# Seven block products in place of eight for six more groups of a SwiGLU layer, in a two-layer trunk on one core

## The chip, the core and the metric

The kernel runs on one core of a Trainium2 chip. Its engines are TensorE (PE; its weight loads are listed apart as PEld), VectorE (DVE), ScalarE (ACT), GpSimd (POOL) and SyncE (SP), which issues most transfers. The metric is the time of one execution in device microseconds (us), lower is better.

## The reference, cut to what matters

Two layers; each is half a SwiGLU, a mixer, half a SwiGLU. The sequence has 256 rows (two tiles of 128), the model 1024 columns, the SwiGLU 2816 hidden columns.

```python
def _swiglu(h, w_gate, w_up, w_down):
    return (jax.nn.silu(h @ w_gate) * (h @ w_up)) @ w_down

for layer in range(DEPTH):
    x = x + 0.5 * _swiglu(_rmsnorm(x, ffn_norm[layer, 0]), ffn_w_gate[layer, 0],
                          ffn_w_up[layer, 0], ffn_w_down[layer, 0])
    h = _rmsnorm(x, mix_norm[layer])
    ...
    x = x + mixed.astype(x.dtype)
    x = x + 0.5 * _swiglu(_rmsnorm(x, ffn_norm[layer, 1]), ffn_w_gate[layer, 1],
                          ffn_w_up[layer, 1], ffn_w_down[layer, 1])
```

So there are four SwiGLUs, which the kernel numbers f = 0 to 3. The mixer behind f = 0 is an attention with rotary tables (cosines and sines of the positions) beside pooling groups.

## The kernel before, in words

**Precision.** Every product is made of three fp32r products: a matrix is split into a high part (ACT copies it to fp32r, `hi_of`) and a low part (DVE subtracts, `tt`), and high x high, high x low and low x high are added in PSUM. So each weight costs ACT one pass and DVE one pass before PE can use it. The splits are written to `wh` and `wl`, a ring of four units (RING); the transfers land in `raw`, four buffers. A unit is half of a group's gate and up columns (512 rows of the model by 256 + 256 columns) or a group's rows of `ffn_w_down`.

**Groups.** The hidden columns go in 11 groups of 256 (g = 0 to 10). For a group, `gate_up` makes for each tile t and each half kh of the model's columns 12 products of 128 x 512 (4 blocks by 3 terms) into one PSUM buffer `wk`; ACT takes the silu (`sg`), DVE multiplies (`pr`). `hid_T` transposes `pr` on PE into a PSUM buffer `sk` and splits it (`hh`, `hl`); `down` adds 12 products for each tile into the accumulators `acc`. `wk` and `sk` have two buffers each. The step of a group (`ffn_joint`) is: four times 12 products of gate and up; `down` of the group before for tile 0; `hid_T`; `down` of the group before for tile 1.

**Pairs.** `ffn_pairs` treats two neighbouring groups together: tiles, halves of the model's columns and the two groups make 2 x 2 blocks, and seven products of blocks (`pair_product`, j = 1, 6, 2, 7, 5, 4, 3 in that order) replace eight. Its rows are sums of blocks of the normalised rows, scaled by `rho` so that both tiles share a scale (`pair_rows`, eight or four passes of DVE), and are transposed by 16 PE transposes (`pair_turn`) into `sTh`, `sTl`. Its weights come raw into `sr` (four buffers, one pair's worth); `split_pair` makes sums and differences of them on DVE (into `sr` and `t2`) and splits the seven results, each in two parts. After each product DVE or ACT adds it into `u`; a gate's result is `pp`. Before, `PAIRS = {3: (2, 5, 8)}`: only f = 3 does this, for groups 2 and 3, 5 and 6, 8 and 9.

**Order.** A scheduler decides the order on each engine from the steps' order and priorities; each engine then runs its list strictly in that order. `opened` (a step behind group 3 of f = 0) loads the mixer's constants and makes the rotary tables, some 58 small DVE instructions (names `rt..`, `rang`, `posf`, `cs`).

Of the kernel before, what the change touches and what calls it, by code (L numbers as in the profile page):

```python
# [17 lines left out]
DM = 1024  # L18
# [21 lines left out]
    p510 m1 t00 p500 v00 t11 p411 p511 G1 p501 v10 G0 t13 v01 v11 V0 V1 o20 o21 o31 o30  # L40
"""

PAIRS = {3: (2, 5, 8)}


ORDER = """
# [66 lines left out]
def trunk_kernel(ctx: ExitStack, tc: tile.TileContext, I, out):  # L113
# [341 lines left out]
    def gate_up(f, g, t, kh, ks):  # L455

        w = held["f", f, g, kh]
        o = slice(t * 128, (t + 1) * 128)
        if (f, g, t) not in gups:
            gups[f, g, t] = wk((128, 2, 256))  # L460
        ps = gups[f, g, t]

        sides = [slice(0, 1), slice(1, 2)] if (f, g, t, kh) == (0, 0, 0, 0) else [slice(0, 2)]
        for sd in sides:
            for x, y in ((hTh, w[0]), (hTh, w[1]), (hTl, w[0])):
                for k in ks:
                    keep("gu", mm(ps[:, sd], x[:, 4 * kh + k, o], y[:, k, sd],
                                  kh == 0 and k == 0 and y is w[0] and x is hTh and sd.start == 0,
                                  kh == 1 and k == 3 and x is hTl))
                if x is hTh and y is w[0]:  # L470
                    pins["up"] = pins["gu"]
        if kh == 0 or ks[-1] != 3:
            return
        del gups[f, g, t]
        sg = tmp.tile([128, 256], F32, tag="t256", name="sg")
        pr = tmp.tile([128, 256], F32, tag="pr256", name="pr")
        with prio(CHAIN):
            ACT.activation(out=sg, in_=ps[:, 0], func=AF.Silu, scale=rstds[f, t])  # L478
            stt(pr, ps[:, 1], rstds[f, t], sg, ALU.mult, ALU.mult)
        prods[f, g, t] = pr  # L480
# [12 lines left out]
    def pair_rows(f):  # L493

        a11, a12, a21, a22 = (hn[t][:, c * 512:(c + 1) * 512] for t in range(2) for c in range(2))
        rho = pr_["rho"]
        if f == 0:
            gv = pr_["pool"].tile([128, DM], F32, name="pg")
            SP.dma_start(out=gv, in_=I["ffn_norm"][0, 0].partition_broadcast(128))
            for t in range(2):  # L500
                for c in range(2):
                    o = slice(c * 512, (c + 1) * 512)
                    tt(hn[t][:, o], xs[t][:, o], gv[:, o], ALU.mult)
        root = pr_["pool"].tile([128, 1], F32, name="root")
# [56 lines left out]
    def hid_T(f, g, *ts):  # L561
# [3 lines left out]
                         hidp.tile([128, 2, 256], F32R, tag="hl", name="hl"))  # L565
        o = slice(ts[0] * 128, (ts[-1] + 1) * 128)
        h, l = (x[:, :, o] for x in hid[f, g])
        ps = sk((128, 2, len(ts) * 128))
        with prio(CHAIN), behind("down" if g else "gu"):
            for n, t in enumerate(ts):  # L570
                pr = prods.pop((f, g, t))
# [16 lines left out]

    at = {}

    def even_open():
        at["pool"] = p = tc.alloc_tile_pool(name="even", bufs=1)
        for nm, c0, n in (("NA", C_NA, 128), ("NB", C_NB, 256),
                          ("corr", C_CR, 64), ("invf", C_IF, 8)):
            at[nm] = p.tile([128, n], F32, name=nm)
            SP.dma_start(out=at[nm], in_=cst[:, c0:c0 + n])
        at["pw"] = p.tile([128, 4, 128], F32, name="pw")
        SP.dma_start(out=at["pw"], in_=I["ev_pool_w"][0].rearrange("g c e -> c g e"))
        at["psc"] = p.tile([128, 4], F32, name="psc")
        SP.dma_start(out=at["psc"], in_=I["ev_pool_scale"][0].rearrange("(g e) -> e g", e=128))  # L600
        at["gqk"] = p.tile([128, 2, 64], F32, name="gqk")
        SP.dma_start(out=at["gqk"][:, 0], in_=I["ev_q_norm"][0].partition_broadcast(128))
        SP.dma_start(out=at["gqk"][:, 1], in_=I["ev_k_norm"][0].partition_broadcast(128))
        at["pos"] = p.tile([128, 2], I32, name="pos")
        SP.dma_start(out=at["pos"], in_=I["positions"][0].rearrange("(t p) -> p t", p=128))
        at["qk"] = [p.tile([128, 2, 8, 64], F32, name=f"qk{t}") for t in range(2)]
        at["v"] = [p.tile([128, 8, 65], F32, name=f"v{t}") for t in range(2)]
        for t in range(2):
# [11 lines left out]
            at[nm] = [p.tile([128, 8], F32, name=f"{nm}{t}") for t in range(2)]  # L620
        at["att"] = [p.tile([128, 8, 64], F32, name=f"att{t}") for t in range(2)]
        at["plT"] = [p.tile([128, 4, 128], F32, name=f"plT{t}") for t in range(2)]
        at["cs"] = p.tile([128, 2, 2, 2, 8], F32, name="cs")
        at["ra"] = p.tile([128, 8, 2, 8], F32, name="ra")
        for nm in ("s8", "r8"):
            at[nm] = [p.tile([128, 8], F32, name=f"{nm}{n}") for n in range(2)]
# [89 lines left out]
        tt(cos, z, u, ALU.mult)  # L716

    def rotary_tables():
        p = at["pool"]
        posf = p.tile([128, 2], F32, name="posf")  # L720
        ang = p.tile([128, 2, 8], F32, name="rang")
        DVE.tensor_copy(out=posf, in_=at["pos"])
# [696 lines left out]
    def ffn_joint(f, g0, g1):  # L1419

        for g in range(g0, g1):
            paced.add(len(steps))
            for kh in range(2):
                if f == 1 and g == NG - 1 and kh:
                    S(hold)
                for t in range(2):
                    GU(f, g, t, kh)
                    if g == 1 and kh == 0:
                        HID(f, 0, t)
                    if g == 1 and f in PAIRS:  # L1430
                        S(lambda n=2 * kh + t: pair_turn(n))
            if g < NG - 1:
                dn(f, g - 1, 0)
# [3 lines left out]
    def ffn_pairs(f, g0, g1):  # L1437

        g = g0
        while g < g1:  # L1440
# [70 lines left out]


    def first():
        row = hn[1][0:8, 0:128]
        with prio(3 * CHAIN):
            ACT.dma_start(out=ident, in_=cst[:, C_ID:C_ID + 128])
# [55 lines left out]
    S(lambda: table(AF.Silu, "hT"))  # L1572
    GU(0, 0, 0, 1)
    GU(0, 0, 1, 1)
    ffn_joint(0, 1, 4)

    def opened():
        with behind("load"):
            load_g("m0", I["mix_norm"][0])
            even_open()  # L1580
        rotary_tables()
    S(opened)
    ffn_joint(0, 4, NG)
    tail(0, N(0, "m0"), HT(0))
    S(lambda: norm(1, "m0"))

# [37 lines left out]
    PO(1, 1, (1,))  # L1624
    C(x_update, 1, None, (1,))
    C(table, AF.Silu)
    S(lambda: at["pool"].release())
    S(s5_open)
    head(1, "f1")
    S(lambda: gens.append(s5_build()))  # L1630
# [144 lines left out]
```

## Time and profile before

| | |
|---|---|
| median of 3 runs | 937.63 us (936.35 to 939.73) |
| the profiled execution | 937.66 us |
| its span, first to last instruction | 935.9 us |
| PE busy | 914.7 us, 98% of the span |
| PEld busy | 755.9 us, 81% |
| DVE busy | 711.3 us, 76% |
| ACT busy | 464.9 us, 50% |
| mean granted TensorE clock | 0.998 of full speed |

Busy time of PE is a sum over pipelined matmuls whose ends are modelled: a matmul's duration overlaps its successor's. How fast PE runs is read from the starts of successive rows. In the rows, an idle time in brackets is what the engine waited before the row, and for whom.

### The profile page before, as it was taken

How to read it: one execution, taken by the hardware profiler on the slowest of the kernel's cores; microseconds unless marked ns; L12 is line 12 of the kernel's file. 1: busy time of each engine (PE TensorE's matmuls, PEld its weight loads, DVE VectorE, ACT ScalarE, POOL GpSimd, SP SyncE). 2: the span in 40 equal slices, each digit the busy share in tenths (PEclk: the TensorE clock that was granted, in tenths of full speed). 3: DMA queues.
4: the chain of work that ended last, by engine and by line, in shares of the span. 5: the costliest groups of instructions: out<-in, count | busy, mean ns of one | idle time of the engine just before them, and what ended most of it. 6: DMA issues, size and time to landing. Idle time of an engine off the chain costs nothing.

```text
span 935.9 us, 13253 instructions
## 1 busy us (share of the span) xinstructions
PE 914.7 (98%) x4981; PEld 755.9 (81%) x4981; DVE 711.3 (76%) x1141; ACT 464.9 (50%) x643; POOL 64.9 (7%) x114
## 2 busy tenths in 40 slices
PE   7999999999999999999999999999879999999998
PEld 5888888889988888888888888888658788887876
DVE  5756654578967659999896557999496689999992
ACT  6544444455536444434454444444345465656561
POOL 0000000013020000000132001600200000000000
PEclk9999999999999999999999999999999999999999
DMA  7867656654476877556788655865956941939141
GB/s 249 276 193 219 192 183 200 193 166 142 134 193 202 197 228 209 174 154 209 235 240 295 191 180 165 250 206 183 301 217 194 333 148 47 335 101 320 53 134 46
DMA packets 149055, 184.59 MB, mean 197 GB/s; under 512 B 23160, under 2 KB 131648, under 8 KB 148224
## 3 DMA queue, kind: packets, MB, share of 16 engines
q1 hardware_dynamic: 145184, 174.70, 60.0%
q0 software_dynamic: 3504, 8.92, 3.8%
q8 instruction: 39, 0.64, 0.3%
q10 hardware_dynamic: 304, 0.14, 0.1%
q14 instruction: 24, 0.20, 0.1%
HBM read 173.24 MB, written 9.44 MB: 195 GB/s over the span
## 4 chain that ended last, share of the span: by engine, by line
PE 76%; DVE 9%; DMA 7%; ACT 3%; issue 3%; POOL 1%; SPq 0%; ACTq 0%; DVEq 0%; POOLq 0%
PE wk L103 46%; PE acc L103 25%; PE sk L103 5%; DMA raw<-in_ffn_w_up_dram 3%; DVE wl L141 3%; DMA raw<-in_s_w_glu_dram 2%; ACT wh L184 1%; DMA V<-x 1%; DVE X L141 1%; DVE b_t L141 1%; POOL r L742 1%; DMA raw<-in_ffn_w_gate_dram 1%; ACT acc L383 0%; ACT h L1211 0%; DVE b_q L141 0%
## 5 line engine op out<-in xcount | busy, mean ns | idle before, releaser
L141 DVE TENSOR_TENSOR wl<-raw,wh 128x1024 fp32r<-128x1024 f32 (+1 forms) x281 | 335.1, 1217 | 119.6 <-ACT wh L184 118.7
L184 ACT ACTIVATE wh<-raw 128x1024 fp32r<-128x1024 f32 (+1 forms) x281 | 285.6, 1051 | 216.0 <-PE wk L103 94.5
L103 PE MATMUL wk<-wh,hTh 128*128 128x512 f32 (+1 forms) x776 | 203.1, 380 | 3.0 <-DVE pr L150 1.5
L103 PE MATMUL wk<-wl,hTh 128*128 128x512 f32 (+1 forms) x776 | 200.2, 377 | 0.0
L103 PE MATMUL wk<-wh,hTl 128*128 128x512 f32 (+1 forms) x776 | 199.4, 376 | 0.0
L103 PEld LDWEIGHTS wk<-wh,hTh 128*128 128x128 f32 x776 | 139.6, 189 | 30.2 <-ACT hTh L184 2.5
L103 PEld LDWEIGHTS wk<-wl,hTh 128*128 128x128 f32 x776 | 140.8, 189 | 26.5 <-DVE wl L141 0.2
L103 PEld LDWEIGHTS wk<-wh,hTl 128*128 128x128 f32 x776 | 140.8, 189 | 26.4
L103 PE MATMUL acc<-wh,hh 128*128 128x512 f32 x352 | 141.4, 402 | 1.4 <-ACT hh L184 1.4
L103 PE MATMUL acc<-wl,hh 128*128 128x512 f32 x352 | 137.2, 390 | 0.0
L103 PE MATMUL acc<-wh,hl 128*128 128x512 f32 x352 | 137.0, 392 | 0.0
L478 ACT ACTIVATE sg<-wk,rstd 128x256 f32<-128x256 f32 x76 | 35.8, 472 | 95.1 <-PE wk L103 90.5
L103 PEld LDWEIGHTS acc<-wh,hh 128*128 128x128 f32 x352 | 66.2, 188 | 14.8 <-ACT hh L184 2.7
L103 PEld LDWEIGHTS acc<-wh,hl 128*128 128x128 f32 x352 | 66.1, 188 | 14.8 <-DVE hl L141 0.7
L103 PEld LDWEIGHTS acc<-wl,hh 128*128 128x128 f32 x352 | 66.3, 188 | 12.4
L150 DVE SCALAR_TENSOR_TENSOR pr<-wk,rstd,sg 128x256 f32<-128x256 f32 x76 | 36.4, 480 | 35.9 <-ACT sg L478 35.9
L141 DVE TENSOR_TENSOR wl<-sr,wh 128x1024 fp32r<-128x1024 f32 x36 | 42.8, 1219 | 2.6 <-ACT wh L184 2.6
L184 ACT ACTIVATE hh<-sk 128x512 fp32r<-128x512 f32 (+1 forms) x52 | 27.4, 527 | 29.6 <-PE sk L103 29.6
L184 ACT ACTIVATE wh<-sr 128x1024 fp32r<-128x1024 f32 x36 | 36.2, 1052 | 11.5 <-PE acc L103 5.2
L141 DVE TENSOR_TENSOR hl<-sk,hh 128x512 fp32r<-128x512 f32 (+1 forms) x52 | 31.3, 604 | 4.3 <-ACT hh L184 4.3
L383 ACT ACTIVATE acc<-x 128x512 f32<-128x512 f32 x24 | 14.3, 597 | 22.6 <-DVE x L150 18.3
L103 PE MATMUL sk<-ident,pr 128*128 128x128 f32 x152 | 24.4, 273 | 0.3 <-DVE pr L150 0.3
(322 smaller groups left out, 819.7 us busy)
## 6 DMA issues: line engine op xcount, KB each, us to landing
raw<-in_ffn_w_down_dram SPq DMA_DIRECT2D x88, 512.0 KB
raw<-in_ffn_w_up_dram SPq DMA_DIRECT2D x76, 512.0 KB
raw<-in_ffn_w_gate_dram SPq DMA_DIRECT2D x75, 512.0 KB
raw<-in_ev_w_in_dram SPq DMA_DIRECT2D x16, 512.0 KB
raw<-in_s_w_glu_dram SPq DMA_DIRECT2D x16, 512.0 KB
sr<-in_ffn_w_gate_dram SPq DMA_DIRECT2D x12, 512.0 KB
sr<-in_ffn_w_up_dram SPq DMA_DIRECT2D x12, 512.0 KB
raw<-in_ev_w_out_dram SPq DMA_DIRECT2D x8, 512.0 KB
```

The lines of the kernel that those rows point to most:

```text
L103: i = f(*a, **k)
L141: return DVE.tensor_tensor(out=o, in0=a, in1=b, op=op)
L150: return DVE.scalar_tensor_tensor(out=o, in0=a, scalar=s, in1=b, op0=op0, op1=op1)
L184: return ACT.activation(out=o, in_=i, func=AF.Copy)
L383: keep("square", ACT.activation(out=into or acc_of(t)[c], in_=xs[t][:, s], func=AF.Square, scale=1.0 / 32.0, accum_out=sums[t][:, c:c + 1]))
L478: ACT.activation(out=sg, in_=ps[:, 0], func=AF.Silu, scale=rstds[f, t])
L742: POOL.tensor_tensor(out=r8, in0=s8, in1=mhalf.to_broadcast([128, 8]), op=ALU.pow)
```

## The change

`PAIRS` gets an entry for f = 0: groups 3 and 4, 6 and 7, 9 and 10 are paired; groups 0, 1, 2, 5 and 8 stay single. `pair_rows(0)` is a step behind group 0, so its instructions lie in groups 0 and 1; the four `pair_turn` of f = 0 lie in group 2. For f = 0 the rows aren't in `hn` as rows, so `pair_rows` loads the norm's gain to all partitions (`gv`, 512 KB, now in the buffer `gvec`) and multiplies again. Group 1's gate and up go to `sk` buffers instead of `wk`, and group 0's `hid_T` to `wk` instead of `sk`. The mixer's constants and rotary tables lie in a pool `even_pre`, made at the start; the mixer's other tiles are opened only when the pair's pool is released. `opened` now stands behind the first pair. Behind the last pair `ffn_pairs` returns before `down`, which `tail` issues.

```diff
-PAIRS = {3: (2, 5, 8)}
+PAIRS = {0: (3,6,9,), 3: (2,5,8,)}
...
-            gups[f, g, t] = wk((128, 2, 256))
+            gups[f, g, t] = (sk if (f, g) == (0, 1) else wk)((128, 2, 256))
...
-            gv = pr_["pool"].tile([128, DM], F32, name="pg")
+            gv = tmp.tile([128, DM], F32, tag="gvec", name="gvec", bufs=1)
...
-        ps = sk((128, 2, len(ts) * 128))
+        ps = (wk if (f, g) == (0, 0) else sk)((128, 2, len(ts) * 128))
...
-    def even_open():
-        at["pool"] = p = tc.alloc_tile_pool(name="even", bufs=1)
+    def even_load():
+        p = at["pre"]
...
-                    if g == 1 and f in PAIRS:
+                    if f in PAIRS and g == PAIRS[f][0] - 1:
                         S(lambda n=2 * kh + t: pair_turn(n))
...
             HID(f, g, 0, 1)
+            if g == NG - 2:
+                return
             dn(f, g, 0)
...
     def first():
+        at["pre"] = tc.alloc_tile_pool(name="even_pre", bufs=1)
+        pair_open(0)
...
-    ffn_joint(0, 1, 4)
+    S(lambda: pair_rows(0))
+    ffn_pairs(0, 1, 5)
...
-            even_open()
+            even_load()
         rotary_tables()
     S(opened)
-    ffn_joint(0, 4, NG)
+    ffn_pairs(0, 5, NG)
+    S(lambda: pr_["pool"].release())
+    S(even_open)
     tail(0, N(0, "m0"), HT(0))
```

**The start of group 1.** On DVE, before, around the end of group 0 (`ss` are the sums for the norm, `wl` with `raw` the low parts of weights, `pr` group 0's results):

```order
L150 SCALAR_TENSOR_TENSOR ss<-ss 128x1 x2
L141 TENSOR_TENSOR wl<-raw,wh 128x4x256
L150 SCALAR_TENSOR_TENSOR pr<-wk,rstd,sg 128x256
L141 TENSOR_TENSOR wl<-raw,wh 128x4x256
L150 SCALAR_TENSOR_TENSOR pr<-wk,rstd,sg 128x256
```

And of the changed kernel:

```order
L150 SCALAR_TENSOR_TENSOR ss<-ss 128x1 x2
L141 TENSOR_TENSOR prho<-rstd,root 128x1
L141 TENSOR_TENSOR prho<-prho,root 128x1
L141 TENSOR_TENSOR h_85<-x_81,gvec 128x512
L141 TENSOR_TENSOR wl<-raw,wh 128x4x256
L150 SCALAR_TENSOR_TENSOR pr<-wk,rstd,sg 128x256 x2
L141 TENSOR_TENSOR wl<-raw,wh 128x4x256 x2
L141 TENSOR_TENSOR hl<-wk,hh 128x2x128
```

Three instructions of `pair_rows` stand ahead of the `wl` behind the sums, which is the second part of group 1's first unit. On PE group 1's products themselves keep their places and write to `sk`.

**The second pair of f = 0.** On DVE of the changed kernel, the tables' small instructions (`rts`, `rtc`, `rtr`, `rtz`) now stand between the second pair's splits (`wl` from `sr`) and the sums of its products (`u`):

```order
L141 TENSOR_TENSOR wl<-sr,wh 128x1024
L141 TENSOR_TENSOR u_96<-wk,u_95 128x512
L150 SCALAR_TENSOR_TENSOR rts<-rts,rtz 128x16
L150 SCALAR_TENSOR_TENSOR rtc<-rtc,rtz 128x16
L141 TENSOR_TENSOR wl<-sr,wh 128x1024
L150 SCALAR_TENSOR_TENSOR rts<-rts,rtr 128x16
L150 SCALAR_TENSOR_TENSOR rtc<-rtc,rtz 128x16
L141 TENSOR_TENSOR wl<-sr,wh 128x1024
L150 SCALAR_TENSOR_TENSOR u_95<-wk,prho,u_95 128x512
```

Before, they stood behind group 3, between the splits of single groups. Of the 58, 27 stand ahead of the first row on the sum `u_96` shown here, 42 ahead of the end of the pair's products.

**The end of the last pair of f = 0.** On PE of the changed kernel, the last product (with `sTh`, `sTl`), the transposes of group 9's second result, and the first `down` products:

```order
L103 MATMUL wk<-wh,sTl 128x512 x4
L103 MATMUL sk<-ident,pp 128x128 x2
L103 MATMUL acc_414<-wh,hh 128x512
L103 MATMUL acc_414<-wl,hh 128x512
L103 MATMUL acc_415<-wh,hh 128x512
L103 MATMUL acc_415<-wl,hh 128x512
```

And DVE at the same place (`u_97` is the product before the last, `u_96` the last):

```order
L141 TENSOR_TENSOR u_97<-wk,u_97 128x512
L141 TENSOR_TENSOR wl<-raw,wh 128x1024
L141 TENSOR_TENSOR u_96<-wk,u_96 128x512
L150 SCALAR_TENSOR_TENSOR pp<-u_97,rstd,sg 128x256
L141 TENSOR_TENSOR wl<-raw,wh 128x1024
L150 SCALAR_TENSOR_TENSOR pp<-u_96,rstd,sg 128x256
L141 TENSOR_TENSOR wl<-raw,wh 128x1024
L141 TENSOR_TENSOR hl<-sk,hh 128x512
```

Before, PE had at the same place, behind group 10's last product, 12 `down` products of group 9 with the transposes between them:

```order
L103 MATMUL wk<-wh,hTl 128x512 x4
L103 MATMUL acc_384<-wh,hh 128x512
L103 MATMUL acc_384<-wl,hh 128x512
L103 MATMUL acc_384<-wh,hl 128x512
L103 MATMUL acc_384<-wh,hh 128x512
L103 MATMUL acc_384<-wl,hh 128x512
L103 MATMUL acc_384<-wh,hl 128x512
L103 MATMUL sk<-ident,pr 128x128 x2
```

Behind the other pairs products of the next single group stand there; behind the last one none is left.

## Rows read from the trace of the kernel before

**Rows 1.** The page's first part: busy time, share of the span, instructions.

```profile
PE 914.7 (98%) x4981; PEld 755.9 (81%) x4981; DVE 711.3 (76%) x1141; ACT 464.9 (50%) x643; POOL 64.9 (7%) x114
```

**Rows 2.** Windows: length, engines' busy us (instructions), clock, DMA share, GB/s.

```profile
core 0: us, PE busy (x) PEld busy (x) DVE busy (x) ACT busy (x) POOL busy (x), PEclk, DMA share, GB/s
20.00:40.85 20.85, 19.38 (x89) 15.58 (x88) 16.03 (x19) 14.46 (x21) 0.88 (x7) 1.00 0.86 273
40.85:91.21 50.36, 50.36 (x229) 41.71 (x228) 27.32 (x41) 22.39 (x27) 0.00 (x0) 1.00 0.69 214
781.01:829.20 48.19, 47.97 (x217) 39.34 (x216) 46.75 (x50) 29.04 (x34) 0.00 (x0) 1.00 0.60 197
829.20:877.47 48.27, 48.01 (x217) 39.26 (x216) 47.34 (x51) 29.38 (x34) 0.00 (x0) 1.00 0.61 196
```

**Rows 3.** Timeline of PE in f = 0: first products of groups 1 and 2.

```profile
23.37 1.21 PE L103 MATMUL wk<-wh,hTh 128*128 128x512 f32 x4 [1.47 <-DVE pr L150]
24.42 1.09 PE L103 MATMUL wk<-wl,hTh 128*128 128x512 f32 x4
...
40.85 1.07 PE L103 MATMUL wk<-wh,hTh 128*128 128x512 f32 x4
41.76 1.07 PE L103 MATMUL wk<-wl,hTh 128*128 128x512 f32 x4
```

**Rows 4.** Timeline of PE in f = 3: one turn between products.

```profile
771.46 0.60 PE L103 MATMUL sk<-ident,h 128*128 128x128 f32 x4
771.81 1.17 PE L103 MATMUL wk<-wh,hTh 128*128 128x512 f32 x4
772.82 1.08 PE L103 MATMUL wk<-wl,hTh 128*128 128x512 f32 x4
```

**Rows 5.** Timeline of DVE at the end of group 0 of f = 0.

```profile
20.74 0.16 DVE L150 SCALAR_TENSOR_TENSOR ss<-ss 128x1 f32<-128x1 f32 x1 [1.29 <-ACT acc L383]
21.69 1.23 DVE L141 TENSOR_TENSOR wl<-raw,wh 128x1024 fp32r<-128x1024 f32 x1 [0.79 <-ACT wh L184]
22.83 0.48 DVE L150 SCALAR_TENSOR_TENSOR pr<-wk,rstd,sg 128x256 f32<-128x256 f32 x1
```

**Rows 6.** Timelines of POOL (f = 0, then f = 3) and DVE (f = 3).

```profile
20.98 0.55 POOL L408 TENSOR_TENSOR rstd<-ss,mhalf 128x1 f32<-128x1 f32 x1 [0.89 <-DVE ss L150]
...
753.50 0.54 POOL L505 TENSOR_TENSOR root<-rstd,mhalf 128x1 f32<-128x1 f32 x1 [0.28 <-POOL rstd L408]
...
754.07 0.16 DVE L141 TENSOR_TENSOR prho<-rstd,root 128x1 f32<-128x1 f32 x1 [1.54 <-POOL root L505]
```

**Rows 7.** Timeline of DVE in the third pair of f = 3.

```profile
886.99 2.36 DVE L141 TENSOR_TENSOR wl<-sr,wh 128x1024 fp32r<-128x1024 f32 x2 [2.10 <-ACT wh L184]
889.26 0.68 DVE L141 TENSOR_TENSOR u<-wk,u 128x512 f32<-128x512 f32 x1
889.86 2.35 DVE L141 TENSOR_TENSOR wl<-sr,wh 128x1024 fp32r<-128x1024 f32 x2
```

**Rows 8.** Timeline of DVE in f = 0: small instructions between two splits.

```profile
94.07 0.17 DVE L150 SCALAR_TENSOR_TENSOR rts<-rts,rtr 128x16 f32<-128x16 f32 x1
94.15 0.17 DVE L150 SCALAR_TENSOR_TENSOR rtc<-rtc,rtz 128x16 f32<-128x16 f32 x1
94.24 1.22 DVE L141 TENSOR_TENSOR wl<-raw,wh 128x1024 fp32r<-128x1024 f32 x1
```

**Rows 9.** Timelines of PE, then DVE, in the first pair of f = 3.

```profile
790.99 1.07 PE L103 MATMUL wk<-wh,sTl 128*128 128x512 f32 x4
...
806.65 0.38 PE L103 MATMUL sk<-ident,pp 128*128 128x128 f32 x2
...
807.72 0.50 PE L103 MATMUL acc<-wh,hh 128*128 128x512 f32 x1 [0.22 <-ACT hh L184]
...
792.09 0.69 DVE L141 TENSOR_TENSOR u<-wk,u 128x512 f32<-128x512 f32 x1 [0.17 <-PE wk L103]
...
805.62 0.48 DVE L150 SCALAR_TENSOR_TENSOR pp<-u,rstd,sg 128x256 f32<-128x256 f32 x1
```

More of the change, by code (lines that the diff above doesn't have):

```diff
@@ L598, in even_open @@
         SP.dma_start(out=at["pw"], in_=I["ev_pool_w"][0].rearrange("g c e -> c g e"))
-        at["psc"] = p.tile([128, 4], F32, name="psc")
+        at["psc"] = p.tile([128, 52], F32, name="psc")[:, 0:4]
         SP.dma_start(out=at["psc"], in_=I["ev_pool_scale"][0].rearrange("(g e) -> e g", e=128))
@@ L605, in even_open @@
         SP.dma_start(out=at["pos"], in_=I["positions"][0].rearrange("(t p) -> p t", p=128))
+        at["cs"] = p.tile([128, 2, 2, 2, 8], F32, name="cs")
+    def even_open():
+        at["pool"] = p = tc.alloc_tile_pool(name="even", bufs=1)
         at["qk"] = [p.tile([128, 2, 8, 64], F32, name=f"qk{t}") for t in range(2)]
@@ L622, in even_open @@
         at["plT"] = [p.tile([128, 4, 128], F32, name=f"plT{t}") for t in range(2)]
-        at["cs"] = p.tile([128, 2, 2, 2, 8], F32, name="cs")
         at["ra"] = p.tile([128, 8, 2, 8], F32, name="ra")
@@ L718, in rotary_tables @@
     def rotary_tables():
-        p = at["pool"]
+        p = at["pre"]
         posf = p.tile([128, 2], F32, name="posf")
@@ L1626, in trunk_kernel @@
     C(table, AF.Silu)
-    S(lambda: at["pool"].release())
+    S(lambda: (at["pool"].release(), at["pre"].release()))
     S(s5_open)
```

## The prediction

> **What bounds the kernel now.** I read the page's busy times first: PE 98% of the span, DVE 76%, PEld 81% [rows 1]. A mean over stages says little, so next came windows of the stages that the change copies from and to [rows 2]. The reader is to see two regimes. Three single groups of f = 0 (from group 2's first product on) take 50.36 us with PE busy throughout and DVE busy 27.32, so PE alone sets the time and a group costs 50.36 / 3 = 16.79 us. In f = 3, a pair and a single group take 48.19 and 48.27 us; PE is idle 0.2 to 0.3 us there, but DVE is busy 46.75 and 47.34 us. There PE still sets the time, with an engine beside it that has no reserve. What the change buys is PE time; what it risks is DVE time. The PE pace is read from starts: four products of 512 columns start 0.91 us apart from the next four (40.85 to 41.76) [rows 3], 0.227 us each.
>
> **The change part by part.**
>
> *The pairs.* A pair has 7 x 12 products where two single groups have 8 x 12: 12 fewer, 12 x 0.227 = 2.72 us. What reaches the end is read from f = 3, which has all that comes with it: 50.36 - 48.19 = 2.17 and 50.36 - 48.27 = 2.09, mean 2.13 us [rows 2]. The missing 0.6 us goes to transposes that break a run of products and to waits for `hh`. I take 2.13 for the pairs 3, 4 and 6, 7: -4.26 us.
>
> The Trainium skill ("TensorE: Matmul & The Clock Gate", section "Wait — 56ns, not 53.3ns?") gives warm matmuls of 512 columns a spacing of 215.7 ns. The trace's 227 ns is 5% above it. By the page the 36 products saved would be worth 7.77 us in place of 8.16, and the total would come out 0.4 us later.
>
> *The last pair, 9 and 10.* The others fill the time behind the last product with the next group's products. Here nothing is left but `down` of group 9, which needs `hh` from the `pp` of the last product but one, and DVE's list puts `u` of the last product ahead of that `pp`. So, from the end of the last product on (E, the place where the next product would start): in f = 3 such a row of four started at 790.99, its successor was due 0.91 later, at 791.90, and DVE's `u` began at 792.09, E + 0.2 [rows 9]. `u` holds DVE 0.60 us (889.26 to 889.86) [rows 7], so `pp` begins at E + 0.8. From a `pp` at 805.62 to the first `acc` at 807.72 are 2.10 us, of which about 0.5 were PE's own queue: the `pp` ended at 806.10, the transposes began at 806.65 [rows 9]. That leaves 1.6, so `acc` starts at E + 2.4; less 0.26 us for two transposes PE is idle 2.1 us. `hl` comes behind two more splits of 1.14 us each and a `pp` of 0.4 (spacings 2.27 / 2 for the splits [rows 7]), about E + 4.6, while PE has eight products without it (1.8 us): another 0.4 us. The last pair gives 2.72 - 2.1 - 0.4 = 0.2 us. Lower bound of that gap 0.2 us (the wait in rows 9), upper 2.6.
>
> *The turns.* Four in group 2. In f = 3 a turn started at 771.46 and the four products behind it ended their turn at 772.82: 1.36 us for four products that take 0.91, so 0.45 each, +1.8 us [rows 4]. Nothing hides them; PE is full there.
>
> *Group 1's banks.* Before, PE waited 1.47 us for `pr`, which frees a `wk` buffer [rows 3]. With `sk` the first four products needn't wait. But the next four need the low part of both halves of the unit, and DVE now does three things first. POOL's second `rstd` ends at 21.53; `root` starts 0.28 later and takes 0.54, and DVE follows at 754.07, 0.03 after the end [rows 6]: 22.4. Two `prho` (0.2 each) and a pass of 512 (0.6) bring 23.3, where the split stood at 21.69 [rows 5]. It ends at 24.5, so PE's low products start at 24.5, where they started at 24.42 [rows 3]. The wait changes its name. I take +0.1 us; the bounds are -1.5 (the wait gone) and +1.9 (the gain's 512 KB, at 273 GB/s [rows 2], just too late).
>
> *Rows made ahead.* Eight passes of 512 on DVE at 0.60 to 0.66 and four `sTl`: about 7.5 us in groups 0 to 2. DVE's list from the `prho` up to the low part that the pair's second product needs has 25 passes of 1024 at 1.14 us, 14 of 512 at 0.60 to 0.66, six `pr` and two short `hl` at 0.4: 40 us, from 22.4 on to 62.7, and with its waits for PE some 65. PE needs that part at 40.85 + 16.79 + 1.8 + 0.1 = 59.5 (the pair's start), plus 12 and 24 products and four more, 9.1 us: 68.6. So 3.6 us are left: 0.
>
> *Rotary tables.* 58 small instructions go from a stretch with DVE half idle to one where it is full. Between splits two of them cost 0.17 us (94.07 to 94.24) [rows 8], so 27 ahead of the second pair's first `u` cost 2.3 us, 42 to the end of the products 3.6. In f = 3 DVE gains on PE from pair to pair: in the third it stood 2.10 us for want of a free weight buffer [rows 7]. The second pair of f = 0 follows a stretch of single groups and should stand as that one; moreover its `u` rows stand one split of 1.14 us earlier than in f = 3's list. 2.3 against 2.10 + 1.14: 0. The cover gone, it would be up to 47.34 + 58 x 0.085 - 48.27 = 4.0 us.
>
> *The rest.* Ten transfers (the next norm's gain and the constants) move on SP behind the first pair. The last of them, the positions, is what the tables start from, with all of DVE behind it; six passes of 1024 and more stand on DVE between the split that lets SP go on and that first instruction, some 9 us for ten issues: 0. The mixer's tiles open late, but its memsets and first writes come after the pair's last reads. The extra 512 KB and the pair's `sr` need about 1 MB more by the pair's start; the DMA share before it is 0.86, then 0.69 [rows 2], which leaves room.
>
> Sum against the profiled execution's 937.66 us (the median of the runs is 937.63): -4.26 - 0.2 + 1.8 + 0.1 = -2.56, **935.1 us**. The part behind f = 0 is the same work and takes over the shift whole.
>
> **The rivals.**
>
> *A: it pays more.* The gain arrives and `rstd` follows sooner, or the last pair's gap is filled. Group 1's wait gone: 935.1 - 1.6 = 933.5; the last pair like the others: 935.1 - 1.9 = 933.2; both: 931.6. For it: group 1's wait is a buffer's, and the buffer is changed. Against it: the list of DVE.
>
> *B: VectorE becomes the bound, and it is slower.* Place: the second pair of f = 0, where 58 small instructions meet a DVE that has 0.9 us in 48 to spare [rows 2]. Its `u` rows free PE's `wk` buffers, so each us of lateness stops PE. If the pair stands like f = 3's second, without the 2.10 us: 935.1 + 4.0 = 939.1. It is slower than before from 2.6 us of overrun on. For it: the DVE rows; against it: the third pair's wait [rows 7].
>
> *C: the start is late.* The first pair's rows or its transfers take more than the 3.6 us left, or the gain stands in the way of group 0's `pr`, with everything of DVE behind it. All of the rows' 7.5 us on the path: 935.1 + 7.5 - 1.8 = 940.8 or more.
>
> *D: the clock.* The gap at the last pair drops TensorE to its lower level. In the trace the clock stayed at 1.00 through the window that holds the wait of 1.47 us [rows 2, 3]; the gap is little longer. If it fell to 1.2 GHz, half the pace, for the 12 products behind the gap, they cost another 2.72: 937.8. The Trainium skill ("TensorE: Matmul & The Clock Gate", section "HAM oscillation — how this bites in real kernels") says that idle gaps re-throttle the array; no run here shows it at this place.
>
> **How the numbers follow.** What a measurement of this kernel can tell from no change is about 0.3%, 2.8 us: faster is below 934.8, slower above 940.5. The forecast has 0.50, with its own range 933.6 to 936.6 (a turn or a gap misjudged by a half); 0.19 of it lies below 934.8. A has 0.24, all faster. B has 0.17, of it 0.04 above 940.5. C has 0.06, slower. D has 0.03, same. Faster 0.43; slower 0.10; same 0.47. The range from 931.8 to 939.3 leaves out C and the ends of A and B, under 2 in 10.
>
> **What would show it.** Starts of PE: group 2 near 40.9, the first pair near 59.5, then 48.2 us to the second and third pair each (48.2 right, 52 is B). A wait of `wk` for `wl` of about 1.5 us in group 1 in place of that for `pr`. A wait of `acc` for `hh` of some 2 us near 178 to 180 us. PE waiting for `u` or `wl` in the second pair is B; a gap ahead of the first pair's second product is C; a clock under 1.00 behind the last pair is D. The prediction is wrong if the last pair's gap is filled, or if DVE's reserve in the second pair isn't that of f = 3's third.

## The result, and the profile after

The changed kernel takes 946.69 us (median of 7 runs, 944.42 to 948.5), the kernel before 938.12 beside it (936.35 to 942.93): ratio 1.0077, 95% interval 1.0055 to 1.010. It is slower by some 8 us, where 2.6 us less was forecast. The profiled execution takes 947.14 us, its span is 945.3.

The page of the changed kernel, its first part, to be read beside [rows 1]:

```profile
PE 913.7 (97%) x4961; PEld 751.9 (80%) x4961; DVE 774.6 (82%) x1218; ACT 487.3 (52%) x668; POOL 66.5 (7%) x115
```

PE is busy 1.0 us less, and the span is 9.4 us longer: PE waits 10.4 us more. The mean granted clock fell too, from 0.998 to 0.994. DVE has 63 us more, as the pairs want. To find the waits, the span is cut at places that both traces have. The timeline of PE in the kernel before has these marks: the mixer's first product, its first score transposes, the first warm-up products behind f = 2, the first wait of the S5 layer, and the second product of f = 3's first pair:

```profile
199.21 0.64 PE L103 MATMUL wk<-wh,hTh 128*128 128x256 f32 x4
...
238.22 0.60 PE L103 MATMUL sk<-ident,sc 128*128 128x128 f32 x4
...
667.64 1.90 PE L103 MATMUL wk<-warm 128*128 128x512 bf16 x8
...
674.88 0.57 PE L103 MATMUL wk<-ident,h 128*128 128x128 f32 x2 [2.13 <-DVE h L141]
...
789.17 1.07 PE L103 MATMUL wk<-wh,sTh 128*128 128x512 f32 x4
```

The timeline of PE in the changed kernel: group 1's wait (answers to [rows 3]), the first products of group 2 and of the first pair, the second product of each of the three pairs, the waits between them, and then the same marks:

```profile
25.77 1.21 PE L103 MATMUL sk<-wl,hTh 128*128 128x512 f32 x4 [1.44 <-DVE wl L141]
...
42.78 1.07 PE L103 MATMUL wk<-wh,hTh 128*128 128x512 f32 x4
...
61.51 1.07 PE L103 MATMUL wk<-wh,hTh 128*128 128x512 f32 x4
...
69.67 1.07 PE L103 MATMUL wk<-wh,sTh 128*128 128x512 f32 x4
...
89.74 0.50 PE L103 MATMUL acc<-wh,hh 128*128 128x512 f32 x1 [2.06 <-ACT hh L184]
...
119.83 1.07 PE L103 MATMUL wk<-wh,sTh 128*128 128x512 f32 x4
...
168.18 1.07 PE L103 MATMUL wk<-wh,sTh 128*128 128x512 f32 x4
...
178.67 0.44 PE L103 MATMUL sk<-ident,pp 128*128 128x128 f32 x2 [1.04 <-DVE pp L150]
...
187.36 0.44 PE L103 MATMUL sk<-ident,pp 128*128 128x128 f32 x2 [1.18 <-DVE pp L150]
...
189.00 0.50 PE L103 MATMUL acc<-wh,hh 128*128 128x512 f32 x1 [1.20 <-ACT hh L184]
...
202.13 0.64 PE L103 MATMUL wk<-wh,hTh 128*128 128x256 f32 x4
...
242.20 0.60 PE L103 MATMUL sk<-ident,sc 128*128 128x128 f32 x4
...
673.52 1.90 PE L103 MATMUL wk<-warm 128*128 128x512 bf16 x8
...
683.65 0.72 PE L103 MATMUL wk<-ident,h 128*128 128x128 f32 x2 [5.01 <-DVE h L141]
...
798.48 1.07 PE L103 MATMUL wk<-wh,sTh 128*128 128x512 f32 x4
```

Windows of the changed kernel, with the columns of [rows 2]: group 2, the first and the second pair (each from its second product to the next pair's), and the last pair up to the mixer:

```profile
42.78:61.51 18.73, 18.73 (x94) 15.48 (x93) 17.12 (x21) 9.73 (x14) 0.00 (x0) 1.00 0.93 319
69.67:119.83 50.16, 48.10 (x217) 39.24 (x216) 47.38 (x71) 29.45 (x35) 0.00 (x0) 1.00 0.66 211
119.83:168.18 48.35, 48.27 (x218) 39.27 (x216) 46.66 (x83) 27.63 (x34) 0.00 (x0) 1.00 0.63 196
160.02:202.13 42.11, 38.17 (x173) 30.56 (x172) 38.88 (x46) 26.46 (x36) 0.84 (x6) 1.00 0.32 101
```

The second pair is what was forecast (48.35). The first lasts as long as the single groups that it replaces, with 2.06 us of PE idle in one wait. The last pair has PE idle 3.9 us.

The cuts give five stages. The first column is the start of the first product of 512 columns (12.91 before); "f = 0 and mixer" goes on to the score transposes, "f = 1, f = 2" to the warm-up products, "S5 layer" to f = 3's second product, "f = 3" to the span's end. The last column is the ratio to the kernel before with its interval.

| us | start | f = 0 and mixer | f = 1, f = 2 | S5 layer | f = 3 | ratio |
|---|---|---|---|---|---|---|
| before | 12.91 | 225.31 | 429.42 | 121.53 | 146.73 | 1 |
| changed | 14.34 | 227.86 | 431.32 | 124.96 | 146.82 | 1.0077 (1.0055 to 1.010) |
| e5_after_again | 12.75 | 230.29 | 431.45 | 125.08 | 146.83 | 1.0054 (1.0032 to 1.0075) |
| e1_pace | 13.24 | 227.29 | 428.97 | 119.97 | 146.93 | 1.0018 (0.9995 to 1.0040) |
| e2_before_pace0 | 13.22 | 225.33 | 432.01 | 124.62 | 146.32 | 1.0042 (1.0025 to 1.0059) |
| e3_two_pairs | 14.61 | 226.83 | 429.28 | 125.69 | 147.79 | 0.9995 (0.9976 to 1.0013) |
| e4_no_rotary | 13.76 | 224.78 | 429.52 | 122.45 | 146.69 | 0.9988 (0.9969 to 1.0006) |
| e6_hh_first | 13.28 | 225.75 | 428.74 | 124.61 | 145.82 | 0.9980 (0.9966 to 0.9993) |
| e7_two_late | 15.54 | 222.40 | 429.29 | 126.00 | 146.97 | 0.9969 (0.9952 to 0.9986) |
| e8_pool_rot | 13.11 | 225.28 | 429.04 | 120.50 | 146.47 | 0.9979 (0.9963 to 0.9995) |
| e9_two_pool | 13.51 | 223.49 | 429.15 | 122.55 | 147.00 | 0.9981 (0.9960 to 1.0002) |
| e10_four_first | 13.27 | 224.18 | 428.81 | 122.38 | 146.06 | 0.9971 (0.9950 to 0.9991) |

Of the 9.4 us, 1.43 are the start, 2.55 f = 0 and the mixer, 1.90 f = 1 and f = 2, and 3.43 the S5 layer. More than half lies where nothing of the change stands. A profile is one execution: the starts of all twelve run from 12.75 to 15.54 (the kernel before's code up to there is in e2, at 13.22), so the 1.43 us lies within the spread; that the change adds nothing there is not shown.

The clock has a part in the S5 layer. Windows of that layer in the kernel before, then in the changed kernel:

```profile
667.64:789.17 121.53, 112.27 (x985) 88.78 (x984) 91.34 (x127) 62.55 (x107) 4.29 (x8) 0.99 0.66 200
```

```profile
673.52:798.48 124.96, 114.36 (x985) 90.14 (x984) 91.48 (x127) 62.97 (x107) 4.29 (x8) 0.96 0.65 194
```

PE's 985 instructions are busy 2.1 us longer, at a granted clock of 0.96 in place of 0.99; the other 1.3 us are waiting. Each execution's mean clock is on record beside its time: on the mean 0.9968 over the 35 executions of the kernel before beside e1 to e4, 0.9941 over the first 7 of the changed kernel and 0.9946 over its 10 in e5. An estimate from these: about 0.0025 x 940 = 2.4 us of the loss at most come with a lower clock.

### The profile page after: what moved, and what is told of

The parts are those of the page before. It is cut to its first block, busy times and chain, and to the rows that moved or that the text cites. A ratio compares the mean times of both kernels' runs of the same rounds, so it can differ in the third digit from the quotient of the medians.

```text
span 945.3 us, 13291 instructions
## 1 busy us (share of the span) xinstructions
PE 913.7 (97%) x4961; PEld 751.9 (80%) x4961; DVE 774.6 (82%) x1218; ACT 487.3 (52%) x668; POOL 66.5 (7%) x115
## 4 chain that ended last, share of the span: by engine, by line
PE 64%; DVE 20%; DMA 7%; issue 3%; ACT 3%; POOL 1%; SPq 0%; ACTq 0%; DVEq 0%; POOLq 0%
PE wk L103 36%; PE acc L103 21%; DVE wl L141 8%; PE sk L103 7%; DMA raw<-in_ffn_w_down_dram 2%; DMA raw<-in_ffn_w_up_dram 2%; DVE X L141 2%; ACT wh L184 1%; DVE b_q L141 1%; POOL r L746 1%; DMA gvec<-in_ffn_norm_dram 1%; DVE sr L141 1%; DVE u L141 1%; DMA V<-x 1%; DVE pr L150 1%
## 5 line engine op out<-in xcount | busy, mean ns | idle before, releaser
L141 DVE TENSOR_TENSOR wl<-raw,wh 128x1024 fp32r<-128x1024 f32 (+1 forms) x257 | 307.4, 1214 | 73.4 <-ACT wh L184 72.7
L184 ACT ACTIVATE wh<-raw 128x1024 fp32r<-128x1024 f32 (+1 forms) x257 | 262.7, 1052 | 196.0 <-PE wk L103 56.6
L103 PE MATMUL wk<-wh,hTh 128*128 128x512 f32 (+1 forms) x700 | 182.9, 379 | 2.8 <-ACT hTh L184 1.4
L103 PE MATMUL wk<-wl,hTh 128*128 128x512 f32 (+1 forms) x700 | 180.4, 376 | 0.0
L103 PE MATMUL wk<-wh,hTl 128*128 128x512 f32 (+1 forms) x700 | 179.5, 375 | 0.8 <-DVE hTl L141 0.8
L103 PEld LDWEIGHTS wk<-wh,hTl 128*128 128x128 f32 x700 | 126.6, 189 | 24.6 <-DVE hTl L141 1.3
L141 DVE TENSOR_TENSOR wl<-sr,wh 128x1024 fp32r<-128x1024 f32 x72 | 85.5, 1216 | 2.9 <-ACT wh L184 2.6
L184 ACT ACTIVATE wh<-sr 128x1024 fp32r<-128x1024 f32 x72 | 72.4, 1052 | 23.2 <-DVE sr L141 9.6
L141 DVE TENSOR_TENSOR sr<-sr 128x1024 f32<-128x1024 f32 x24 | 28.7, 1214 | 0.0
L103 PE MATMUL wk<-wl,sTh 128*128 128x512 f32 x96 | 26.5, 392 | 0.0
```

Of the source, the lines that this page charges most:

```text
L103: i = f(*a, **k)
L141: return DVE.tensor_tensor(out=o, in0=a, in1=b, op=op)
L184: return ACT.activation(out=o, in_=i, func=AF.Copy)
```

## The experiments

**Why anything behind f = 0 changes.** The S5 layer's preparation is a generator that is advanced a step at a time between the products of f = 1 and f = 2. Its pace is a counter that also runs where no generator is there yet:

```python
def run_gens():
    state["credit"] += PACE
    while state["credit"] >= 1.0:
        state["credit"] -= 1.0
        for g in list(gens):
            ...
```

It is called once for each single group and for each of 36 `down` steps of f = 0. Ten single groups make 46 calls; four (1, 2, 5, 8) make 40. With PACE = 0.8 that leaves 36.8, or 0.8 over, before, and 32.0, or 0.0 over, after. So the preparation's steps land at other places in f = 1 and f = 2. My first theory was that this phase costs the time behind f = 0; the rival was buffers and memory in other places, or a lucky profile.

*e1_pace.* The changed kernel with the counter put back:

```diff
+CREDIT = 0.8
...
-    S(lambda: gens.append(s5_build()))
+    S(lambda: (gens.append(s5_build()), state.update(credit=CREDIT)))
```

> The changed kernel, with the counter that paces the S5 layer's preparation set to 0.8 where that preparation starts, the value that it has there in the kernel before (in the changed kernel it is 0.0). With it the order of every engine behind f = 0 is that of the kernel before, row for row. Theory (the counter's phase makes the work behind f = 0 worse): the loss behind the mixer's score transposes goes, which is 703.1 - 697.7 = 5.4 us from the trace of after (span 945.3, transposes at 242.20) and of before (935.9, 238.22); the time is 946.7 - 5.4 = 941.3, ratio 1.0034, and f = 0 still ends about 4 us late. Rival (the work behind f = 0 is slower because its buffers and memory lie elsewhere, or because the profile of before was a lucky one): 946 to 947.

*e2_before_pace0.* The kernel before with the counter of the changed kernel:

```diff
+CREDIT = 0.0
...
-    S(lambda: gens.append(s5_build()))
+    S(lambda: (gens.append(s5_build()), state.update(credit=CREDIT)))
```

> The kernel before, with nothing of the change but the counter: 0.0 in place of 0.8 where the S5 layer's preparation starts. Theory: slower than before by the whole loss behind f = 0, 5.4 us: 943.5, ratio 1.0057, with VectorE's h waiting for the gain some 2 us ahead of f = 2 and TensorE waiting about 5 us in place of 2.1 at the S5 layer's start. Rival (buffers and memory, not order): 938.

e1 came to 1.0018 (0.9995 to 1.0040), which holds the 1.0034 expected and excludes the rival's 946 to 947 us; e2 came to 1.0042: the counter alone, with nothing else of the change, makes the kernel before slower by 3.9 us (0.0042 x 940; 2.3 to 5.5). That is less than the 5.4 expected, which was read from one profile of each kernel, and excludes the rival's 938. In e2's timeline of DVE the wait that the changed kernel has ahead of f = 2 is there:

```profile
473.90 1.29 DVE L142 TENSOR_TENSOR h<-x,gvec 128x512 f32<-128x512 f32 x2 [2.25 <-DMA gvec<-in_ffn_norm_dram]
```

The changed kernel's own row, from its timeline of DVE, where the kernel before had no wait for the gain:

```profile
476.80 1.29 DVE L141 TENSOR_TENSOR h<-x,gvec 128x512 f32<-128x512 f32 x2 [2.16 <-DMA gvec<-in_ffn_norm_dram]
```

The gain is late because SP comes to it late. Timelines of SP, the kernel before and then the changed kernel:

```profile
460.03 0.58 SPq L354 DMA_DIRECT2D gvec<-in_ffn_norm_dram  x1
```

```profile
469.56 0.51 SPq L354 DMA_DIRECT2D gvec<-in_ffn_norm_dram  x1
```

SP issues it 9.5 us later, where the kernel had lost some 3.5 until then; in e2 it does so at 466.56. In the table f = 1 and f = 2 split cleanly: 428.74 to 429.52 in the nine profiles with 0.8, 431.32 to 432.01 in the three with 0.0, 2.5 us apart on the mean. The S5 layer doesn't: 124.62 to 125.08 with 0.0, but 119.97 to 126.00 with 0.8, with the time at which the transfers `V<-x` land and with the clock. Part of e2's loss lies there too, but no profile can say how much. The executions' mean clock is 0.9948 in e2, 0.9968 in the kernel before beside it, so up to 1.9 us of the 3.9 (0.0020 x 940, an estimate) come with a lower clock.

*e5_after_again.* The changed kernel once more, on the chip of the three runs that follow.

> The changed kernel as it is, on one chip with the runs that follow. Theory (f = 0 and the mixer cost 2.0 us, as in the first experiment's stages: 187.25 - 186.30 and 40.04 - 39.01; the counter costs the rest): 2.0 + 3.9 us, the second being what the counter alone cost the kernel before; ratio 1.006. Rival (the loss of 8.6 us of the first comparison is all of the code): ratio 1.009.

Ratio 1.0054 (1.0032 to 1.0075): the theory's 1.006 lies within, the rival's 1.009 outside. This profile has something that the first one hasn't. Windows of e5:

```profile
core 0: us, PE busy (x) PEld busy (x) DVE busy (x) ACT busy (x) POOL busy (x), PEclk, DMA share, GB/s
...
88.00:90.00 2.00, 2.00 (x9) 1.60 (x8) 2.00 (x3) 1.06 (x1) 0.00 (x0) 0.78 1.00 367
90.00:92.00 2.00, 2.00 (x6) 1.61 (x5) 2.00 (x3) 1.70 (x2) 0.00 (x0) 0.50 0.60 182
...
188.00:190.00 2.00, 1.60 (x4) 1.31 (x5) 2.00 (x4) 1.41 (x2) 0.00 (x0) 0.53 0.52 176
190.00:192.00 2.00, 2.00 (x7) 1.55 (x6) 2.00 (x2) 0.74 (x1) 0.00 (x0) 0.62 0.76 222
```

Behind both gaps (the wait for `hh` ends at 87.62 here, after 2.02 us) the granted clock goes to 0.50, which is 1.2 GHz. The first dip costs 2 x 0.22 + 2 x 0.50 = 1.4 us in these rows, the second up to 2 x 0.47 + 2 x 0.38 = 1.7 (PE stands 0.4 us of it), and f = 0 and the mixer take 230.29 in place of 227.86, 2.4 more. The first profile has the same gaps and 1.00 behind them. The Trainium skill ("TensorE: Matmul & The Clock Gate", section "HAM oscillation — how this bites in real kernels") says that idle gaps between bursts of matmuls take TensorE to the lower clock, and describes longer gaps; here 2.02 us, and 2.4 in two parts, were enough in one execution and not in the other.

*e3_two_pairs.* As e1, with the last pair taken out:

```diff
-PAIRS = {0: (3,6,9,), 3: (2,5,8,)}
+PAIRS = {0: (3, 6), 3: (2,5,8,)}
```

> As the first run (counter at 0.8), with the last pair taken out: groups 9 and 10 singly, pairs 3, 4 and 6, 7 as they are. Theory (the last pair costs more than it saves: from its first product to the mixer's first the trace of after loses 1.28 us on before, and 1.05 more inside the mixer, by VectorE's debt): 941.3 - 1.3 - up to 1.05 = 939 to 940. Rival (the prediction's own term, the last pair saves 0.2): 941.5.

Ratio 0.9995, 939.2 us, as the theory had it; the mixer fell back to 39.0 (241.44 less its first product at 202.44). The profile of this run had a dip of the clock behind the first pair's gap (0.50 from 92 to 94), so f = 0 as a whole doesn't price the last pair. What lies behind the dip does: from the second pair's second product to the score transposes e3 takes 121.69 to 241.44, 119.75 us, and e1 118.18 to 240.53, 122.35. The last pair costs e1 2.6 us.

*e4_no_rotary.* As e1, the tables' 58 DVE instructions left out:

```diff
-        rotary_tables()
+        POOL.memset(at["cs"], 0.5)
```

> As the first run (counter at 0.8, three pairs), with the 58 small VectorE instructions of the rotary tables left out: one memset on GpSimd fills the tables, so the mixer computes with other tables. Theory (VectorE never catches up between the first pair and the last, so these 5 us stand ahead of the third pair's u and pp): the waits for pp at the last pair shrink, and the time falls by 1 to 3 us, to 938.5 to 940. Rival (the tables lie beside other work, as the prediction has it): 941.3.

f = 0 and the mixer went from 227.29 to 224.78, 2.5 us. The time doesn't come out where the tables stand. From the third pair's second product to the mixer's first, e1 takes 166.23 to 200.49, 34.26, and e4 166.56 to 198.90, 32.34: 1.9 of the 2.5 us come out at the last pair, whose first wait (176.62 in e1) begins 23 us behind the tables' last instruction (153.11). In e4's timeline of DVE, third pair, stands a wait that the changed kernel doesn't have there:

```profile
167.91 2.36 DVE L142 TENSOR_TENSOR wl<-sr,wh 128x1024 fp32r<-128x1024 f32 x2 [2.11 <-ACT wh L185]
```

But e4 changed one thing more: at the last pair its scheduler put the `pp` of the last product but one ahead of the last `u` (183.85 and 184.25), where e1 has the `u` first (184.15, then 184.76). So the 2.5 us are a price of the tables and of this order together; e3 and e9, and e6 and e8, below, price the tables at less.

*e6_hh_first.* In the changed kernel's timeline of ACT at the end of the first pair, the split of a weight of group 5 stands ahead of `hh`, and waits for its transfer:

```profile
88.14 1.06 ACT L184 ACTIVATE wh<-raw 128x1024 fp32r<-128x1024 f32 x1 [2.86 <-DMA raw<-in_ffn_w_gate_dram]
89.11 0.58 ACT L184 ACTIVATE hh<-sk 128x512 fp32r<-128x512 f32 x1
```

In f = 3 `hh` stood ahead of it and PE waited 0.22 [rows 9]. The timeline of ACT in the kernel before, first pair of f = 3:

```profile
807.07 0.60 ACT L184 ACTIVATE hh<-sk 128x512 fp32r<-128x512 f32 x1 [1.89 <-PE sk L103]
...
808.50 1.06 ACT L184 ACTIVATE wh<-raw 128x1024 fp32r<-128x1024 f32 x1 [0.43 <-DMA raw<-in_ffn_w_gate_dram]
```

e6 is e1 with that split held back until `hh` is issued:

```diff
+            if late.get(units[i], -1) >= state["step"]:
+                break
...
-            with behind("split"):
+            with behind("split", *(["hh"] if units[i] in late else [])):
```

> The first experiment (three pairs, counter at 0.8) with one order changed: the split of group 5's second unit is made to stand behind the first pair's hh on ScalarE, where the changed kernel has it ahead. Theory (ScalarE stands on a transfer and hh stands behind it, which is TensorE's wait of 1.8 to 2.1 us at the end of the first pair): that wait falls to some 0.3, f = 0 from its first 512-column product to the mixer's first takes 187.25 - 1.6 = 185.7 us, ratio 1.0018 - 0.0017 = 1.000. Rival (VectorE is the bound there, and the time comes back as a wait for pp or hl): 187.2, ratio 1.002.

The timeline of ACT in e6:

```profile
85.27 0.60 ACT L185 ACTIVATE hh<-sk 128x512 fp32r<-128x512 f32 x1 [1.50 <-PE sk L104]
86.45 1.06 ACT L185 ACTIVATE wh<-raw 128x1024 fp32r<-128x1024 f32 x1 [0.58 <-DMA raw<-in_ffn_w_gate_dram]
```

PE's wait there is gone (below 0.2), and the time from the first pair's second product to the second's fell from 49.91 to 48.14: that is the price of the split ahead of `hh`, 1.8 us.

The ratio fell by 0.0038 (1.0018 to 0.9980), 3.6 us, and the profile's f = 0 and mixer by 1.5 (227.29 to 225.75). Two more things in this profile stand between the two. The last pair became faster as well, though the edit doesn't touch it: from its second product to the mixer's first e1 took 34.26, e6 32.16. The scheduler's list has the last `pp` and `u` the other way round there. Timelines of DVE, the changed kernel and then e6:

```profile
186.22 0.69 DVE L141 TENSOR_TENSOR u<-wk,u 128x512 f32<-128x512 f32 x1 [0.28 <-PE wk L103]
186.83 0.47 DVE L150 SCALAR_TENSOR_TENSOR pp<-u,rstd,sg 128x256 f32<-128x256 f32 x1
```

```profile
182.09 0.48 DVE L151 SCALAR_TENSOR_TENSOR pp<-u,rstd,sg 128x256 f32<-128x256 f32 x1
...
183.62 0.68 DVE L142 TENSOR_TENSOR u<-wk,u 128x512 f32<-128x512 f32 x1
```

PE's two waits behind the last product, 1.18 and 1.20 in e1, are one of 0.51 in e6. So the 3.6 us are those of both orders, and not of `hh` alone. And the mixer takes 42.01 where it took 40.04: a wait of 1.44 for `qk`, 0.59 in e1, with a dip of the clock behind it. Timeline of PE and windows of e6:

```profile
205.87 0.76 PE L104 MATMUL wk<-wh,hTh 128*128 128x256 f32 x4 [1.44 <-DVE qk L142]
```

```profile
206.00:208.00 2.00, 2.00 (x12) 2.00 (x13) 1.93 (x7) 0.00 (x0) 0.59 (x1) 0.60 0.95 315
208.00:210.00 2.00, 2.00 (x12) 2.00 (x12) 0.92 (x2) 0.00 (x0) 1.08 (x1) 0.55 0.34 121
```

The four rows of four products behind that wait start 0.85 us apart, where the next ones start 0.48 apart, so the dip cost 1.5 us. Without it the profile would have gained some 3.0, near the 3.6 of the ratio.

*e7_two_late.* As e3, with e6's edit for both pairs, and the constants and tables behind the second pair:

```diff
-    ffn_pairs(0, 1, 5)
+    ffn_pairs(0, 1, 8)
...
-    ffn_pairs(0, 5, NG)
+    ffn_pairs(0, 8, NG)
```

> Two pairs (3, 4 and 6, 7), counter at 0.8, hh ahead of that split in both pairs, and the rotary tables behind the second pair, where groups 8 to 10 run singly. Theory: no wait above 0.5 us is left in f = 0 behind group 1, so 186.3 - 2 x 2.13 + 1.94 for the turns + 0.4 = 184.4 us from the first 512-column product to the mixer's first, mixer 39.0: 2 us under before, ratio 0.998. Rival (VectorE is the bound in the pairs whatever stands there): 186 or more, ratio 1.000.

222.40 us and ratio 0.9969 (0.9952 to 0.9986): it beats both kernels, the one before by 0.3%. It has three edits at once, and how much each gave is not shown. No wait of PE over 0.52 us is left in f = 0 behind group 1. The start was the latest of all (15.54), of which group 0 makes some up; the score transposes stand at 237.94, against 238.22 before.

*e8_pool_rot.* As e6, with `hh` ahead in each pair, and the tables' instructions on GpSimd (a fused one there as two); the line that says so:

```diff
-        angle_tables(p, ang.rearrange("p t f -> p (t f)"), 16, cosv, sinv, "rt")
+        angle_tables(p, ang.rearrange("p t f -> p (t f)"), 16, cosv, sinv, "rt", POOL)
```

> Three pairs, counter at 0.8, hh ahead of the split in each pair, and the rotary tables on GpSimd in place of VectorE (65 instructions there, which is idle in f = 0). Theory (the tables cost 2.1 us in f = 0 and 0.4 in the mixer as in the fourth experiment, the order on ScalarE 1.1 to 2): 185.14 - 1.5 = 183.6 us, mixer 39.6; ratio 0.998. Rival (small instructions on GpSimd slow VectorE beside them, or the mixer waits for the tables): 186 or more, ratio 1.001.

225.28 where 183.6 + 39.6 = 223.2 was expected, and ratio 0.9979. Beside e6 (225.75 and 0.9980, each profile with one dip in this stretch) the tables on VectorE cost half a us or nothing (e8 also has `hh` ahead in the second pair, where e1's PE did not wait for it). The rival's reason, that VectorE is slowed, doesn't hold. Groups of the second pair's stretch in e1, then in e8 (mean ns of one behind the comma):

```profile
L142 DVE TENSOR_TENSOR wl<-sr,wh 128x1024 fp32r<-128x1024 f32 x12 | 14.5, 1217 | 0.0
```

```profile
L142 DVE TENSOR_TENSOR wl<-sr,wh 128x1024 fp32r<-128x1024 f32 x12 | 14.3, 1220 | 0.5 <-ACT wh L185 0.5
```

1217 and 1220 ns: VectorE isn't slower beside GpSimd. GpSimd is. Timelines of DVE, then of POOL, in e8:

```profile
117.86 2.38 DVE L142 TENSOR_TENSOR wl<-sr,wh 128x1024 fp32r<-128x1024 f32 x2 [0.54 <-ACT wh L185]
...
123.03 0.74 DVE L151 SCALAR_TENSOR_TENSOR u<-wk,prho,u 128x512 f32<-128x512 f32 x1
```

```profile
119.12 1.20 POOL L672 TENSOR_TENSOR rtr<-rtw,rtr 128x16 f32<-128x16 f32 x1
...
123.18 0.22 POOL L672 TENSOR_TENSOR rtr<-rtw,rtr 128x16 f32<-128x16 f32 x1
```

The same small instruction takes 1.20 us beside a split, which has both inputs in the on-chip memory, and 0.22 beside a `u`, which has one of them in PSUM: it ends with the split. The mixer didn't wait for the tables, so this cost nothing here. What is left is the last pair: its gap at 182 to 184 and a clock of 0.72 and 0.50 in the 4 us behind it (1.6 us).

*e9_two_pool.* e8 without the last pair:

```diff
-PAIRS = {0: (3,6,9,), 3: (2,5,8,)}
+PAIRS = {0: (3, 6), 3: (2,5,8,)}
```

> The eighth experiment without its last pair: groups 9 and 10 singly, everything else the same (tables on GpSimd, counter at 0.8, hh ahead). It is the price of the last pair alone. Theory (the last pair costs, by its gap, the clock behind the gap and the mixer): 183.4 us from the first 512-column product to the mixer's first and 39.0 in the mixer, as in the seventh, 222.4 together where the eighth has 225.3; ratio 0.997. Rival (the prediction's term, the last pair saves 0.2): 225.5, ratio 0.998 to 0.999.

223.49 against 225.28, where 222.4 was expected: the last pair costs 1.8 us with the tables out of its way, 1.6 of it the clock in that one profile; the ratios, 0.9981 and 0.9979, don't tell the two apart. That it saves anything, no run shows. e9 also prices the tables without a last pair: from the second pair's second product to the mixer's first it takes 116.95 to 198.01, 81.06, and e3, with them on VectorE, 121.69 to 202.44, 80.75. There they cost nothing.

*e10_four_first.* e8 with the last pair's product 4 ahead of 5:

```diff
-            for j in (1, 0, 6, 2, 7, 5, 4, 3):
+            for j in (1, 0, 6, 2, 7, 4, 5, 3) if g == NG - 2 else (1, 0, 6, 2, 7, 5, 4, 3):
...
-                tt(u3, ps, u3, ALU.add)
-                gate(f, g, 1, u3)
+                z = s1 if g == NG - 2 else u3
+                tt(z, ps, u3, ALU.add)
+                gate(f, g, 1, z)
```

> The eighth experiment with the last pair's products in another order: 4 ahead of 5 (its sum goes to another buffer, so that 5 still finds what it needs), so both pp of group 9 come one product earlier, 2.7 us. Theory (what the last pair lacks is down's hh behind the last product; nothing else is late): the two waits of 0.79 and 0.91 us and the lower clock behind them go; 185.6 - 1.7 - 1.7 = 182.2 us, mixer 39.7, together 221.9; ratio 0.996. Rival (VectorE is the bound at the last pair, so the gap only moves to another wait): 225, ratio 0.998.

Its timeline of PE, from the last pair to the mixer:

```profile
187.11 0.41 PE L104 MATMUL sk<-ident,pp 128*128 128x128 f32 x2 [0.87 <-DVE pp L151]
...
196.63 1.29 PE L104 MATMUL sk<-ident,h 128*128 128x128 f32 x8 [1.29 <-DVE h L151]
198.52 0.74 PE L104 MATMUL wk<-wh,hTh 128*128 128x256 f32 x4 [0.60 <-ACT hTh L185]
```

The gap behind the last product is gone, and so is the dip; of the 3.4 us hoped for, 1.1 arrived (225.28 to 224.18). The rest moved to group 10's `pp` and to the `h` ahead of the mixer, which VectorE makes: the rival is right in part. Ratio 0.9971; with e6 to e9 it is one group that this measurement doesn't tell apart.

## Why the prediction was wrong, step by step

The sum of f = 0 and the mixer was forecast at -2.56 and measured at +2.55 in the profile:

| term | forecast | measured | from |
|---|---|---|---|
| turns, four in group 2 | +1.8 | +1.94 | 18.73 - 16.79 |
| group 1 and its banks | +0.1 | +0.50 | (42.78 - 14.34) - (40.85 - 12.91) |
| pairs 3, 4 | -2.13 | -0.20 | 50.16 - 50.36 |
| pairs 6, 7 | -2.13 | -2.01 | 48.35 - 50.36 |
| last pair | -0.2 | +1.26 | 42.11 - (199.21 - 158.36) |
| mixer | 0 | +1.06 | 40.07 - 39.01 |
| all behind it | 0 | +5.42 | 1.90 + 3.43 + 0.09 |

**Right.** The turns; the wait of group 1, which kept its length and changed its name (1.44 for `wl`, where 1.47 for `pr` stood); the rows made ahead (61.51 to 69.67 without a gap, so rival C fell); the second pair at f = 3's pace.

**"The part behind f = 0 is the same work and takes over the shift whole"** failed, and is the largest part. The work is the same; its order isn't. It rested on no row, and the change takes six single groups, each a step of the counter, out of f = 0. Shown: 2.5 us in f = 1 and f = 2, and 3.9 in all by e2, the lower clock included.

**Pairs 3 and 4 at f = 3's price** failed by one instruction on another engine: ScalarE's list has a split that waits for its transfer ahead of `hh`. The price was read from a stretch where it stood behind. e6 shows it: with the split behind `hh` the pair takes 48.14 us, the forecast's 48.2, where it took 49.91.

**Rotary tables, 0.** The pair that they stand in did run at 48.35, so rival B fell at its place, and without a last pair they cost nothing (e3 and e9). But the working was wrong: it set the 27 instructions ahead of the first `u`, 2.3 us, against the 2.10 us of [rows 7], and a wait is a cover only once. The cover was there: the third pair of e4, without the tables, has a wait of 2.11 us, that of e8 one of 2.00. In the changed kernel the tables have filled it, and all 58 of them count, 58 x 0.085 = 4.9 us. VectorE goes into the last pair without a reserve. What that costs lies between half a us or nothing (e6 beside e8) and 2.5 (e4, which changed the order of the last pair too); which part is the lateness and which the order stays open.

**The last pair, -0.2** failed by its size: it costs 2.6 us in e1 beside e3. The gap itself came out near the forecast, 1.18 + 1.20 = 2.4 us idle behind the last product where 2.1 was said. That rests in part on luck: the changed kernel has the order that was read, `u` ahead of `pp`, but with the other order the waits there are 0.51 (e6), 1.49 (e4) and 1.70 us (e8). Put at nothing were the wait ahead of the gap (1.04 at 178.67) and the mixer behind it (40.07, 39.00 in e3); in some executions the clock comes on top, rival D, which also came at a place that D didn't name, the first pair's gap.

## What to carry to other kernels

A stretch that a change doesn't touch is the same work only if its order is the same: compare the order of every engine to the end of the program, and look for counters that run through the changed part. A price read from a sister stretch holds only with its neighbours' order; ahead of each wait that sets the pace, see what stands in front of it on the engine that ends it, and whether that waits for a transfer. A wait that serves as cover can be spent once: set against it everything that comes into the stretch, and look at the next place where the other engine has nothing queued. And an experiment's edit can change the order elsewhere, as e6's did at the last pair: compare all of the order before its result is called the price of one thing.

## What the runs showed of the hardware that was not expected

The same code, with the same gaps of about 2 us in front of PE, ran on at full clock in one profile and at 0.50 for some 3 us in another. Shorter waits did it too, 1.44 us in e6's mixer and 0.79 and 0.91 in e8's last pair, while the wait in group 1, 1.17 to 1.50 us, was followed by no dip in any of the twelve profiles. Such a gap is a price with a chance, and a dip cost 1.4 to 1.7 us where it was read.

Small instructions on GpSimd beside a full VectorE cost VectorE nothing (1217 and 1220 ns); GpSimd pays. The Trainium skill ("GPSIMD Engine Reference", section "1. Specifications") says that the two share their interfaces to the on-chip memory and contend where VectorE has two inputs there. The splits have two, and the trace agrees on GpSimd's side: 0.22 us became 1.20 beside a split. It was busy 43.0 us with 62 instructions (110 to 160 us of e8), 0.69 us each on the mean, where VectorE's stand 0.085 us apart [rows 8].

What stays open is the S5 layer: the same order gave 119.97 and 126.00 us, with the wait for `V<-x` between 3.25 and 6.57 and the clock under 0.95 from 676 to 682 us in e1 and from 676 to 686 in e6; what sets them no run here tells.
